# Moving the last block of transposes behind the u projection, and nine weight sums from GpSimd to VectorE, in a hybrid encoder layer on one Trainium2 core

## The chip, the cores and the metric

The kernel runs on one core of one Trainium2 chip. A core has a matrix engine (TensorE, PE in the profile; PEld is its weight load), a vector engine (VectorE, DVE), a scalar engine (ScalarE, ACT), a programmable engine (GpSimd, POOL) and a sync engine (SyncE, SP) whose queue issues the weight transfers. Each engine works through its own queue in program order, and waits there for what its next instruction needs. The metric is the time of one launch on the device in microseconds (us).

## What is computed

One layer of an encoder, for one sequence of 512 positions and 1024 channels in fp32; the feed-forward width is 2816.

```
h  = rmsnorm(x, g_pre_mix)
q, k, v, g, u, sv, a_ret, a_sgu = split(h @ w_in)       # widths 512 512 1024 1024 1024 1024 1024 1024
o  = layernorm(retention_forward(q, k, v) + retention_backward(q, k, v))
ret = (o * silu(g)) @ w_ret_o
sv = layernorm(gelu(sv));  mixed = w_spatial @ sv (chunks of 128) + b_spatial
sgu = (gelu(u) * mixed) @ w_sgu_o
x1 = x + rmsnorm((sigmoid(a_ret) * ret + sigmoid(a_sgu) * sgu) @ w_out, g_post_mix)
hid = conv3(rmsnorm(x1, g_pre_ffn) @ w_up) + conv_b;  a, b = split(hid)
out = x1 + rmsnorm((gelu(a) * b) @ w_down, g_post_ffn)
```

## The kernel before

**Precision.** Every fp32 matmul is done as three matmuls on halves: `split` makes a high part by an ACT copy (L95) and the low part by a DVE subtraction (L102), and PE multiplies high by high, high by low and low by high. Weights and activations both go through it. A weight block arrives as a raw tile (512 KB, SP's queue, four buffers tagged `raw`), and its high and low parts go into one of nine slots (tag `w4`). `w_get` takes the next unit of a list, `units`, and issues the transfers and splits of the following units ahead of their use, as far as its look-ahead allows.

**Stages.** The wide groups (`t_group`, L541 to L543) come first and make q, k, v, sv and g with the positions on the partitions. The last of them makes the second half of g; `g_evac(acc, 1)` applies Silu to it and multiplies it into the second half of the retention output, `o_sb[t, 1]`, four row blocks of 128 positions (DVE, L676). `last_turn` then transposes these: 16 transposes of 128x128 on PE (L685) into four PSUM banks, row block by row block, with two matmuls in between that sum the spatial weights over a row (L688, into `rws`). ACT and DVE split each bank into `gh` and `gl`, the second half of the left operand of the product with `w_ret_o`.

**The u stage.** Then come four pairs of output blocks for u, class `Pair`. A pair makes a 2x2 arrangement of half blocks with seven products in place of eight, from weights named B11, B21, T1, T2, T3, T4 and B22 and activations x (two halves) and the sums S1 to S4, which are made once. The weights' sums are T1 = B11 + B12 and T3 (DVE, L178 and L179, named by their lines in the profile), T2 = T1 + B22 (GpSimd, L180) and T4 = T2 + B21 (GpSimd, L182). Each of the seven products is twelve matmuls of 128x256 (L756). `part1` issues x·B11, x·B21, S1·T1 and S2·T2, with T2's product accumulating on B11's bank after ACT has copied that bank out; `part2` issues S3·T3, on the same bank again after a further copy; `part3` issues the remaining two. `part3` of a pair is issued after `part1` of the next pair. DVE combines the results (L773, L778, L784, L793, L796, L798), and ACT applies Gelu (L799). The first pair's first product is ordered behind `last_turn`'s last instruction by `tc.issue_after(turned)`.

**Behind it.** `gated_pair` makes a further pair with Sigmoid, `a_ret`, and two whole blocks (`f_block`, L229 to L231) of the product with `w_ret_o`, eight steps of three matmuls of 128x512 each; the steps five to eight read the last `gh` and `gl`. The fourth u pair's `part3` is issued after the first gated pair's `part1`.

**The up-projection.** Later the feed-forward's up-projection runs in couples: a pair and two whole blocks. The pair's T2 and T4 are GpSimd's as above; the results go through the convolution (L1028, L1031, L1035) and the Gelu (L1042).

The order within each engine's queue is made by a scheduler from the program's order and its dependences, and `tc.issue_after` adds an order on one engine.

Of the kernel before, what the change touches and what calls it, by code (L numbers as in the profile page):

```python
# [13 lines left out]
ALU = mybir.AluOpType  # L14

P = 128
D = 1024
S = 512
NT = S // P
# [8 lines left out]
U0, GATE0, GATE1 = 32, 40, 72  # L28
# [8 lines left out]
UP0 = DOWN0 - 2 * NF  # L37
EARLY = 4
COUPLES = [(i, i + 1) for i in range(4, 20, 2)]
# [8 lines left out]
def tile_block(ctx: ExitStack, tc, xT, x, wall, par, cs, wsp, bsp, gpost, gffn, out):  # L48
    nc = tc.nc
# [6 lines left out]
    def nm(s):  # L56
        uid[0] += 1
        return f"{s}_{uid[0]}"

    def blk(dt=F32, n="blk", shape=(P, S)):  # L60
        return sb.tile(list(shape), dt, tag="blk", bufs=NBLK, name=nm(n))
# [17 lines left out]
    def tmp(n="tmp", shape=(P, S)):  # L79
        return sb.tile(list(shape), F32, tag="tmp", bufs=6, name=nm(n))  # L80
# [7 lines left out]
    def ps(shape=(P, S)):  # L88
        return pp.tile(list(shape), F32, tag="ps", name=nm("ps"))

    def const(n, shape):
        return sb.tile(list(shape), F32, tag=n, bufs=1, name=n)

    def copy(o, i):
        return nc.scalar.activation(out=o, in_=i, func=AF.Copy)  # L95

    def as32(t):
        return t.bitcast(F32)

    def split(hi, lo, src):  # L100
        copy(hi, src)
        nc.vector.tensor_sub(lo, src, as32(hi))  # L102
# [6 lines left out]
    units = []  # L109
    i = 0  # L110
    while i < NW:
        pair = [(f, i) for f in FORMS]
        if U0 <= i < GATE0:
            units += pair
            i += 2
        elif GATE0 <= i < GATE1:
            units += pair[:4] + [("blk", i + 2)] + pair[4:] + [("blk", i + 3)]
            i += 4
        elif i == UP0 + 2 * COUPLES[0][0]:
            for a, b in COUPLES:  # L120
                pair = [(f, UP0 + 2 * a) for f in FORMS]
                units += pair[:4] + [("blk", UP0 + 2 * b)] + pair[4:] + [("blk", UP0 + 2 * b + 1)]
            i = UP0 + 2 * COUPLES[-1][1] + 2
        elif i == DOWN0:
            for _ in range(2):
                pairs = [[("q", i + j), ("t", i + j)] for j in range(DP)]
                whole = [[("blk", i + DP)], [("blk", i + DP + 1)]]
                for u in pairs[:4] + whole[:1] + pairs[4:6] + whole[1:] + pairs[6:] if i == DOWN0 else pairs + whole:
                    units += u
                i += DP + WHOLE // 2  # L130
        else:
            units.append(("blk", i))
            i += 1
    w_ready, w_pos, w_held, w_raw = {}, [0, 0], [0], {}

    def raw_tile():
        return sb.tile([P, 1024], F32, tag="raw", bufs=4, name=nm("raw"))
# [4 lines left out]
    def slot(n, at=0, w=1024):  # L142
        return sb.tile([P, 1088], F32R, tag="w4", bufs=9, name=nm(n))[:, at : at + w]
# [23 lines left out]
    def w_form(form, i):  # L167

        if form == "B11":
            a, b = raw_tile(), raw_tile()  # L170
            nc.sync.dma_start(a, wall[i])
            nc.sync.dma_start(b, wall[i + 1])
            w_raw["B11"], w_raw["B12"] = a[:, :S], a[:, S:]
            w_raw["B22"], w_raw["B21"] = b[:, :S], b[:, S:]
        elif form == "T1":
            t = raw_tile()
            w_raw["T1"], w_raw["T2"], w_raw["T3"], w_raw["T4"] = t[:, :S], t[:, S:], w_raw["B12"], t[:, S:]
            nc.vector.tensor_add(w_raw["T1"], w_raw["B11"], w_raw["B12"])  # L178
            nc.vector.tensor_add(w_raw["T3"], w_raw["B12"], w_raw["B22"])  # L179
            nc.gpsimd.tensor_tensor(out=w_raw["T2"], in0=w_raw["T1"], in1=w_raw["B22"], op=ALU.add)  # L180
        elif form == "T4":
            nc.gpsimd.tensor_tensor(out=w_raw["T4"], in0=w_raw["T2"], in1=w_raw["B21"], op=ALU.add)  # L182
        w = slot("wf", 0, 1088)
        lo, hi = w[:, AT_64 : AT_64 + S], w[:, S + AT_192 : 2 * S + AT_192]
        split(hi, lo, w_raw[form])
        return hi, lo
# [50 lines left out]
    T0, T1 = slice(0, 256), slice(256, 512)  # L237
# [88 lines left out]
    for k in range(KD):  # L326
# [10 lines left out]
        if k == 0:  # L337
            for half in range(2):
                for f in (T0, T1) if half == 0 else (slice(0, S),):
                    for a, b in ((wh, xh), (wl, xh), (wh, xl)):  # L340
                        for m in range(4 * half, 4 * half + 4):
                            nc.tensor.matmul(  # L342
                                qk[m][:, f], a[:, m * P : (m + 1) * P], b[0][:, f],
                                start=a is wh and b is xh and f.start == 0, stop=False, skip_group_check=True,
# [27 lines left out]
    ident = const("ident", [P, P])  # L372
# [14 lines left out]
    for t in range(NT):  # L387
        for n in range(2):
# [3 lines left out]
                out=xt, in_=xt, func=AF.Square, accum_out=ss[:, 4 * n + t : 4 * n + t + 1]  # L392
# [10 lines left out]
    v = nc.vector  # L403
# [9 lines left out]
    for c in range(19, 1, -2):  # L413
        v.scalar_tensor_tensor(
            out=lc, in0=lc, scalar=1.0 / c, in1=lb, op0=ALU.add, op1=ALU.mult
        )
    v.scalar_tensor_tensor(out=lc, in0=lc, scalar=1.0, in1=la, op0=ALU.add, op1=ALU.mult)
    with behind():
        v.tensor_scalar(out=lg, in0=lgt, scalar1=0.0, scalar2=None, op0=ALU.min)
    v.scalar_tensor_tensor(  # L420
        out=lg, in0=lc, scalar=-2.0, in1=lg, op0=ALU.mult, op1=ALU.add
# [5 lines left out]
    for m in range(8):  # L427
        t = blk(n="qkraw")
# [8 lines left out]
    for t in range(NT):  # L437
# [4 lines left out]
            start=True,  # L442
            stop=True,
# [120 lines left out]
    o_sb = {}  # L564
# [107 lines left out]
    def g_evac(acc, nh):  # L672
        for t in range(NT):
            g = tmp("g")
            nc.scalar.activation(out=g, in_=acc[t], func=AF.Silu, scale=rstd[:, t : t + 1])
            v.tensor_mul(o_sb[t, nh], o_sb[t, nh], g)  # L676
        if nh == 0:
            transposed([o_sb[t, nh] for t in range(NT)], ogh, ogl)

    def last_turn():  # L680

        p, rw = [ps() for _ in range(4)], ps()
        for t in range(NT):
            for f in range(4):
                i = nc.tensor.transpose(p[f][:, t * P : (t + 1) * P], o_sb[t, 1][:, f * P : (f + 1) * P], ident)  # L685
            if t > 1:
                with tc.issue_after(i.ins):
                    i = nc.tensor.matmul(rw, ones, wst_parts[t - 2], start=t == 2, stop=t == 3)  # L688
        for f in range(4):
            h_, l_ = blk(F32R, "gh"), blk(F32R, "gl")  # L690
            split(h_, l_, p[f])
            ogh.append(h_)
            ogl.append(l_)
        copy(rws, rw)
        return i.ins

# [14 lines left out]
    ones, one = blk(F32R, "ones", (P, P)), blk(n="one", shape=(P, P))  # L711
# [3 lines left out]
    wst_parts = blk(F32R, "wsth"), blk(F32R, "wstl")  # L715
    split(*wst_parts, wst)
    rws = lo64("rws", F32)
    for n, acc in enumerate(t_group()):
        if n < 2:
            for k in (n + 2, n + 6):  # L720
                t = tmp("xT")
# [2 lines left out]
            x_forms(n + 2)  # L724
    sv_norm()
    g_evac(acc, 1)
    turned = last_turn()

    def f_block(ah, al, n, between=None):

# [9 lines left out]
    class Pair:  # L740
# [8 lines left out]
        def product(self, b, act, first, w=None):  # L749
            wh, wl = w or w_get()  # L750
            o = self.b[b][:, T0]
            for k in range(4):
                c = slice(k * P, (k + 1) * P)
                h_, l_ = act(k)
                for n, (w_, a_) in enumerate(((wh, h_), (wh, l_), (wl, h_))):
                    nc.tensor.matmul(  # L756
                        o, w_[:, c], a_, start=first and k == n == 0, stop=k == 3 and n == 2,
                        skip_group_check=True,
                    )
            return o  # L760
# [4 lines left out]
        def s(self, n):  # L765
            return lambda k: self.forms[n][k]

        def part1(self):
            c0, c1 = self.t
            o = self.product(0, self.x(0, T0), True)  # L770
            copy(c0[:, T0], o)
            o = self.product(1, self.x(4, T0), True)
            v.tensor_add(c0[:, T0], o, c0[:, T0])  # L773
            self.product(2, self.s("S1"), True)
            o = self.product(0, self.s("S2"), False)
            copy(c1[:, T0], o)
            if self.scale is not None:
                v.tensor_mul(c0[:, T0], c0[:, T0], self.scale[:, T0])  # L778

# [24 lines left out]
    uT, late = [], None  # L804
    U_HOMES = [lambda: lo64("u", F32), lambda: hi192("u", F32)] + [lambda: blk(n="u")] * 2 + [lambda: hi192("u", F32)] * 4
    for j in range(KD // 2):
        p = Pair(AF.Gelu_apprx_tanh, lambda: U_HOMES.pop()(), None, rbc)
        with tc.issue_after(turned) if j == 0 else ExitStack():
            p.part1()
        if late:  # L810
            late.part3()
        p.part2()
        late = p
        uT += p.t
# [32 lines left out]


    def gated_pair(ah, al, late=None):
        p = Pair(AF.Sigmoid, lambda: tmp("sig"), None, rbc)  # L850
        p.part1()
        if late:
            late.part3()
        o = [f_block(ah, al, KD)]
        p.part2()
        o.append(f_block(ah, al, KD, p.part3))
        return zip(o, p.t)

    r = []
    for j in range(KD // 2):  # L860
        for o, t in gated_pair(ogh, ogl, late if j == 0 else None):
            b = (lo64("r", F32) if j == 0 else hi192("r", F32) if j < 3 else blk(n="r"))
            v.tensor_mul(b, o, t)
            r.append(b)
        mix(2 * j)
        mix(2 * j + 1)
    mh, ml = [], []
    for j in range(KD // 2):
        for i, (o, t) in enumerate(gated_pair(yh, yl)):
            v.tensor_mul(t, o, t)  # L870
            nc.gpsimd.tensor_tensor(out=t, in0=t, in1=r[2 * j + i], op=ALU.add)
            h_, l_ = blk(F32R, "mh"), blk(F32R, "ml")
# [141 lines left out]
    rows2, _ = turn(2, zs[2])  # L1014
    for e in range(1, EARLY):
        early(e, 0)
    _, last3 = turn(3, zs[3])
# [88 lines left out]
    i = 0  # L1106
    while i < NF:
        if i in couples:
            p = Pair(None, lambda: tmp("c"), (h2h, h2l, h2forms))
            p.part1()  # L1110
            o = [f_block(h2h, h2l, KD)]
# [5 lines left out]
        else:  # L1117
            o = []
# [50 lines left out]
    late = list(range(EAGER, DP))  # L1169
# [20 lines left out]
    for j in range(DP):  # L1190
# [5 lines left out]
        if j in (3, 5):  # L1196
            w = w_get()
# [214 lines left out]
```

## Time and profile before

| what | value |
|---|---|
| median of 3 runs | 823.45 us |
| lowest, highest | 822.37, 824.98 us |
| the profiled execution | 821.76 us |
| its span in the trace | 820.0 us |
| its mean granted TensorE clock | 0.998 |
| u stage, last wide matmul to first gated block | 211.8 to 259.2 us |

The span is the time from the first to the last instruction in the trace; the profiled execution's own time lies 1.8 us above it. All positions in the text are microseconds from the span's start. In a row of a timeline stand the start, the length, the engine, the line, the operation, the tiles written and read, the shape and the number of instructions in the row; what follows in brackets is the engine's idle time before it and what ended that. A row of several instructions runs from the first one's start to the last one's end. Matmuls overlap in a pipeline, so a single one's length (0.28 us for 128x256) is more than its share of the time: the distance between starts tells that.

### The profile page before, as it was taken

To read this page: it belongs to the slowest core of one execution; us is meant where nothing else is said; L and a number is where in the kernel's file an instruction comes from. 1 tells how busy PE (TensorE), PEld (TensorE's weight loads), DVE (VectorE), ACT (ScalarE), POOL (GpSimd) and SP (SyncE) were. 2 spreads that over 40 slices of the span, in tenths; PEclk is the share of its full clock that TensorE was granted. 3 is DMA by queue.
4 is the path that set the end of the run, shared out by engine and by line. 5 is a ranking of instruction groups with operands and counts; after the bars stand their busy time and mean duration, and the time that the engine had idled before them with its cause. 6 is when DMAs were issued, how large, how long until landed. Compare 5 with 4: busy or idle time off the path is not lost.

```text
span 820.0 us, 13286 instructions
## 1 busy us (share of the span) xinstructions
PE 809.1 (99%) x5158; PEld 729.0 (89%) x5158; DVE 661.7 (81%) x1107; ACT 441.0 (54%) x777; POOL 101.6 (12%) x102
## 2 busy tenths in 40 slices
PE   9999999999999999999999999999999999999996
PEld 7888888888899999999988898889999998999996
DVE  7489898778898777767765559898889989997967
ACT  6636445536665444444445676565656666555531
POOL 0010000102221111132211210210201200000001
PEclk9999999999999999999999999999999999999999
DMA  8733222212223332233359111333333351223344
GB/s 293 251 116 109 72 78 78 77 53 78 97 97 130 104 104 93 88 103 104 113 164 339 45 56 57 104 103 104 103 104 103 103 181 52 78 104 104 107 151 155
DMA packets 29647, 93.24 MB, mean 114 GB/s; under 512 B 3536, under 2 KB 4432, under 8 KB 29584
## 3 DMA queue, kind: packets, MB, share of 16 engines
q1 hardware_dynamic: 27360, 86.76, 31.6%
q0 software_dynamic: 1360, 4.46, 1.5%
q10 hardware_dynamic: 864, 1.18, 0.4%
q8 instruction: 40, 0.66, 0.3%
q14 instruction: 23, 0.19, 0.1%
HBM read 88.19 MB, written 4.19 MB: 113 GB/s over the span
## 4 chain that ended last, share of the span: by engine, by line
PE 89%; DVE 7%; ACT 2%; issue 1%; DMA 1%; POOL 0%; DVEq 0%; SPq 0%; ACTq 0%; POOLq 0%
PE ps L756 19%; PE ps L230 11%; PE ps L229 11%; PE ps L231 11%; PE ps L1145 11%; PE ps L542 5%; PE ps L541 5%; PE ps L543 5%; PE ps L1161 2%; DVE wf L102 2%; PE ps L903 2%; PE ps L902 2%; PE ps L901 2%; PE ps L826 1%; PE ps L342 1%
## 5 line engine op out<-in xcount | busy, mean ns | idle before, releaser
L102 DVE TENSOR_TENSOR wl<-raw,wh 128x1024 fp32r<-128x1024 f32 (+1 forms) x92 | 107.4, 1175 | 45.5 <-PE ps L756 20.4
L95 ACT ACTIVATE wf<-raw 128x512 fp32r<-128x512 f32 x140 | 84.9, 626 | 100.1 <-PE ps L230 39.7
L102 DVE TENSOR_TENSOR wf<-raw,wf 128x512 fp32r<-128x512 f32 x140 | 112.1, 811 | 20.4 <-ACT wf L95 19.4
L756 PE MATMUL ps<-sh,wf 128*128 128x256 f32 x640 | 119.3, 277 | 1.2 <-ACT c L95 1.0
L95 ACT ACTIVATE wh<-raw 128x1024 fp32r<-128x1024 f32 (+2 forms) x96 | 93.4, 983 | 39.9 <-DMA raw<-wall 16.8
L756 PEld LDWEIGHTS ps<-sh,wf 128*128 128x128 f32 x640 | 100.9, 188 | 2.5 <-ACT c L95 1.2
L230 PE MATMUL ps<-h2l,wh 128*128 128x512 f32 (+1 forms) x256 | 92.6, 363 | 0.0
L229 PE MATMUL ps<-h2h,wh 128*128 128x512 f32 (+1 forms) x256 | 92.6, 364 | 0.0
L231 PE MATMUL ps<-h2h,wl 128*128 128x512 f32 (+1 forms) x256 | 92.4, 362 | 0.0
L756 PE MATMUL ps<-sl,wf 128*128 128x256 f32 x320 | 88.5, 276 | 0.0
L541 PE MATMUL ps<-wh,xh 128*128 128x512 f32 x192 | 75.0, 391 | 0.0
L542 PE MATMUL ps<-wl,xh 128*128 128x512 f32 x192 | 74.9, 390 | 0.0
L543 PE MATMUL ps<-wh,xl 128*128 128x512 f32 x192 | 74.8, 390 | 0.0
L180 POOL TENSOR_TENSOR raw<-raw,raw 128x512 f32<-128x512 f32 x20 | 36.7, 1835 | 236.6 <-DVE raw L178 208.4
L756 PEld LDWEIGHTS ps<-sl,wf 128*128 128x128 f32 x320 | 60.1, 188 | 0.6
L1145 PE MATMUL ps<-dl,fh 128*128 128x256 f32 x216 | 59.8, 277 | 0.0
L1145 PE MATMUL ps<-dh,fh 128*128 128x256 f32 x216 | 59.7, 277 | 0.0
L1145 PE MATMUL ps<-dh,fl 128*128 128x256 f32 x216 | 59.7, 277 | 0.0
L231 PEld LDWEIGHTS ps<-h2h,wl 128*128 128x128 f32 x256 | 48.1, 188 | 7.7
L229 PEld LDWEIGHTS ps<-h2h,wh 128*128 128x128 f32 x256 | 47.8, 188 | 7.1 <-ACT h2h L971 0.3
L230 PEld LDWEIGHTS ps<-h2l,wh 128*128 128x128 f32 x256 | 48.1, 188 | 6.6
L756 PE MATMUL ps<-xh,wf 128*128 128x256 f32 x288 | 53.5, 278 | 0.0
(314 smaller groups left out, 2045.3 us busy)
## 6 DMA issues: line engine op xcount, KB each, us to landing
raw<-wall SPq DMA_DIRECT2D x144, 512.0 KB, 3.6
x<-x SPq DMA_DIRECT2D x24, 256.0 KB, 5.8
x<-x POOLq DMA_DIRECT2D x8, 256.0 KB, 2.3
xT<-xT SPq DMA_DIRECT2D x7, 256.0 KB, 5.3
xT<-xT POOLq DMA_DIRECT2D x4, 256.0 KB, 3.6
out<-zg SPq DMA_DIRECT2D x4, 256.0 KB, 2.0
raw<-wall SPq DMA_DIRECT2D x3, 256.0 KB, 4.8
out<-zs ACTq DMA_DIRECT2D x3, 256.0 KB, 3.8
```

Source lines behind the costliest of these rows:

```text
L95: return nc.scalar.activation(out=o, in_=i, func=AF.Copy)
L102: nc.vector.tensor_sub(lo, src, as32(hi))
L180: nc.gpsimd.tensor_tensor(out=w_raw["T2"], in0=w_raw["T1"], in1=w_raw["B22"], op=ALU.add)
L229: nc.tensor.matmul(o, ah, bh, start=start, stop=False, skip_group_check=skip)
L230: nc.tensor.matmul(o, ah, bl, start=False, stop=False, skip_group_check=skip)
L231: nc.tensor.matmul(o, al, bh, start=False, stop=stop, skip_group_check=skip)
L541: nc.tensor.matmul(acc[t], xh[k][:, c], wh[:, f], start=k == 0, stop=False)
L542: nc.tensor.matmul(acc[t], xh[k][:, c], wl[:, f], start=False, stop=False)
L543: nc.tensor.matmul(acc[t], xl[k][:, c], wh[:, f], start=False, stop=k == KD - 1)
L756: nc.tensor.matmul(o, w_[:, c], a_, start=first and k == n == 0, stop=k == 3 and n == 2, skip_group_check=True,)
L901: nc.tensor.matmul(o, ah, bh, start=k == 0, stop=False)
L1145: nc.tensor.matmul(o, a_[:, c], w_[:, f], start=j == t == i == 0, stop=j == DP - 1 and i == 2 and n not in (M2, M3, M4), skip_group_check= ...
```

## The change

There are three edits. The turn: the two weight sums (`row_sums`) alone follow the last wide group, and u's first product is ordered behind them; the transposes and their splits come in two parts, `last_turn((0, 1))` behind the fourth u pair's `part2`, and `last_turn((2, 3))` behind the first gated pair's `part1`, before the fourth u pair's `part3`. The first pair: its B21 product is issued after T2's, and its units are listed in that order. The sums: T2 and T4 of the four u pairs, and T2 of the first up-projection couple, are DVE's. The engines' instruction counts stay as they were, but for these nine sums, which leave GpSimd for DVE.

```
         if U0 <= i < GATE0:
-            units += pair
+            units += [pair[n] for n in (0, 2, 3, 1, 4, 5, 6)] if i == U0 else pair
...
-            nc.gpsimd.tensor_tensor(out=w_raw["T2"], in0=w_raw["T1"], in1=w_raw["B22"], op=ALU.add)
+            eng = nc.vector if i < GATE0 or i == UP0 + 2 * COUPLES[0][0] else nc.gpsimd
+            eng.tensor_tensor(out=w_raw["T2"], in0=w_raw["T1"], in1=w_raw["B22"], op=ALU.add)
         elif form == "T4":
-            nc.gpsimd.tensor_tensor(out=w_raw["T4"], in0=w_raw["T2"], in1=w_raw["B21"], op=ALU.add)
+            eng = nc.vector if i < GATE0 else nc.gpsimd
+            eng.tensor_tensor(out=w_raw["T4"], in0=w_raw["T2"], in1=w_raw["B21"], op=ALU.add)
...
-    def last_turn():
+    def last_turn(fs):
 
-        p, rw = [ps() for _ in range(4)], ps()
-        for t in range(NT):
-            for f in range(4):
-                i = nc.tensor.transpose(p[f][:, t * P : (t + 1) * P], o_sb[t, 1][:, f * P : (f + 1) * P], ident)
-            if t > 1:
-                with tc.issue_after(i.ins):
-                    i = nc.tensor.matmul(rw, ones, wst_parts[t - 2], start=t == 2, stop=t == 3)
-        for f in range(4):
+        for f in fs:
+            p = ps()
+            for t in range(NT):
+                i = nc.tensor.transpose(p[:, t * P : (t + 1) * P], o_sb[t, 1][:, f * P : (f + 1) * P], ident)
             h_, l_ = blk(F32R, "gh"), blk(F32R, "gl")
-            split(h_, l_, p[f])
+            split(h_, l_, p)
             ogh.append(h_)
             ogl.append(l_)
+        return i.ins
+
+    def row_sums():
+
+        rw = ps()
+        for n, w in enumerate(wst_parts):
+            i = nc.tensor.matmul(rw, ones, w, start=n == 0, stop=n == 1)
         copy(rws, rw)
         return i.ins
...
-    turned = last_turn()
+    summed = row_sums()
...
-        def part1(self):
+        def part1(self, apart=False):
+
             c0, c1 = self.t
+
+            def second():
+                o = self.product(1, self.x(4, T0), True)
+                v.tensor_add(c0[:, T0], o, c0[:, T0])
+
             o = self.product(0, self.x(0, T0), True)
             copy(c0[:, T0], o)
-            o = self.product(1, self.x(4, T0), True)
-            v.tensor_add(c0[:, T0], o, c0[:, T0])
+            if not apart:
+                second()
             self.product(2, self.s("S1"), True)
             o = self.product(0, self.s("S2"), False)
             copy(c1[:, T0], o)
+            if apart:
+                second()
...
-        with tc.issue_after(turned) if j == 0 else ExitStack():
-            p.part1()
+        with tc.issue_after(summed) if j == 0 else ExitStack():
+            p.part1(j == 0)
...
     def gated_pair(ah, al, late=None):
+
         p = Pair(AF.Sigmoid, lambda: tmp("sig"), None, rbc)
-        p.part1()
         if late:
-            late.part3()
+            with tc.issue_after(late.last.ins):
+                turned = last_turn((0, 1))
+            with tc.issue_after(turned):
+                p.part1()
+            with tc.issue_after(p.last.ins):
+                turned = last_turn((2, 3))
+            with tc.issue_after(turned):
+                late.part3()
+        else:
+            p.part1()
```

`product` keeps its last matmul as `self.last` for these orders.

More of the change, by code (lines that the diff above doesn't have):

```diff
@@ L755, in product @@
                 for n, (w_, a_) in enumerate(((wh, h_), (wh, l_), (wl, h_))):
-                    nc.tensor.matmul(
+                    self.last = nc.tensor.matmul(
                         o, w_[:, c], a_, start=first and k == n == 0, stop=k == 3 and n == 2,
```

## The prediction

> **What bounds the kernel now.** I read the page's busy times and its chain first, then the busy windows of the stretches that the change touches, then the timelines of single engines there.
>
> ```profile
> span 820.0 us, 13286 instructions
> ## 1 busy us (share of the span) xinstructions
> PE 809.1 (99%) x5158; PEld 729.0 (89%) x5158; DVE 661.7 (81%) x1107; ACT 441.0 (54%) x777; POOL 101.6 (12%) x102
> ...
> PE 89%; DVE 7%; ACT 2%; issue 1%; DMA 1%; POOL 0%; DVEq 0%; SPq 0%; ACTq 0%; POOLq 0%
> ```
>
> PE is busy for 809.1 of 820.0 us and carries 89% of the chain. The change adds no matmul and takes none away, so it can win only moments in which PE stands still, and lose only by making new ones. All that can be won is therefore small. The question is which stalls lie where the edits reach. The windows (time, PE, PEld, DVE, ACT, POOL busy, granted clock, DMA share, GB/s) show the u stage whole, ten us of it, and the stretch around the first couple:
>
> ```profile
> 211.80:259.20 47.40, 46.93 (x403) 46.08 (x402) 42.34 (x66) 30.62 (x58) 10.28 (x7) 1.00 0.32 106
> 230.00:240.00 10.00, 10.00 (x90) 10.00 (x90) 9.89 (x16) 6.66 (x13) 2.60 (x3) 1.00 0.32 107
> ...
> 508.00:525.00 17.00, 15.98 (x95) 14.01 (x94) 14.63 (x24) 8.61 (x15) 4.71 (x2) 1.00 0.18 56
> ```
>
> The granted clock is 1.00 in each, so the clock explains nothing here. VectorE (DVE) is close behind PE: 9.89 of 10 us in the middle of the u stage. That makes it the engine to watch when sums are moved to it. "Busy" for PE hides stalls under a microsecond, because overlapping records count as busy; I therefore compare start times. First the turn (start, length, instruction, wait):
>
> ```profile
> 211.81 1.47 PE L685 MATMUL ps<-ident,o 128*128 128x128 f32 x12
> 213.04 0.48 PE L688 MATMUL ps<-wsth,ones 128*128 128x512 f32 x1
> 213.79 0.65 PE L685 MATMUL ps<-ident,o 128*128 128x128 f32 x4 [0.27 <-DVE o L676]
> 214.20 0.48 PE L688 MATMUL ps<-wstl,ones 128*128 128x512 f32 x1
> 214.52 0.28 PE L756 MATMUL ps<-xh,wf 128*128 128x256 f32 x1
> ...
> 219.98 0.28 PE L756 MATMUL ps<-xh,wf 128*128 128x256 f32 x1
> ```
>
> From 214.52 to 219.98 there are 48 matmuls of 128x256 (four products of twelve): 0.114 us each. Twelve transposes take 213.04 - 211.81 = 1.23 us, 0.103 each. A weight sum streams 512 columns where a product's matmul streams 256, so I put it at twice 0.114, 0.23 us. The u stage has 16 transposes, 2 sums and 384 product matmuls: 1.64 + 0.46 + 43.7 = 45.8 us. It takes 47.40, so no more than 1.6 us can be won there, whatever the mechanism.
>
> **The change part by part: the turn.** Before, it fills 211.81 to 214.52, 2.71 us, for 1.64 + 0.46 = 2.10 us of work: 0.61 us is standing still, most of it until DVE has multiplied the last row block of o (0.27 shown as a wait, 0.75 between starts where a sum needs 0.23). After, the two sums stand alone behind the last wide product, and u's first product starts at about 211.81 + 0.46 = 212.3. The 16 transposes come back at the end of the stage, when o has long been ready; they cost their 1.64 us again, and two more changes between transposes and products. The change at 214.20 cost 0.32 - 0.23 = 0.09 us, so two cost up to 0.2. Gain 0.4 to 0.6 us; I take **0.45**. The wait for o is not replaced: what the first product now needs is its weights and a bank that ScalarE (ACT) has evacuated, and both came before 214.52 without a wait in the row; whether they come before 212.3 the row does not say, so the lower bound is a loss of this gain.
>
> **The second product put behind T2.** The pair's accumulating bank must be copied out by ACT between S2·T2 and the next product on it. These are the places where PE waits for that copy, and the copies:
>
> ```profile
> 220.21 0.39 PE L756 MATMUL ps<-xh,wf 128*128 128x256 f32 x2
> 220.62 0.38 PE L756 MATMUL ps<-sh,wf 128*128 128x256 f32 x1
> ...
> 244.66 0.28 PE L756 MATMUL ps<-sh,wf 128*128 128x256 f32 x1
> 245.12 0.38 PE L756 MATMUL ps<-sh,wf 128*128 128x256 f32 x1 [0.18 <-ACT u L95]
> ```
>
> ```profile
> 220.18 0.38 ACT L95 ACTIVATE u<-ps 128x256 f32<-128x256 f32 x1 [0.73 <-PE ps L756]
> ...
> 244.69 0.37 ACT L95 ACTIVATE u<-ps 128x256 f32<-128x256 f32 x1
> ```
>
> At 220.62 the first pair loses 0.41 - 2 x 0.114 = 0.18 us, and the restarted matmul is 0.10 longer than its 0.28: 0.28 in all. Four matmuls of the second pair already stood in between and hid the rest. With the whole B21 product there, 12 x 0.114 = 1.37 us cover a copy of 0.38 that starts at once: **0.28** goes. But T2 itself now comes one product earlier after B11, whose copy it needs; one product (S1·T1, 1.37 us) remains between them. That covers 0.38 us unless the copy is held up in ACT's queue by a us. T1's and T2's weights are wanted one product earlier too, and the list of units moves them up by as much.
>
> **The sums on VectorE.** How a GpSimd (POOL) sum stands to DVE's work is seen in a pair of views, POOL's timeline and DVE's:
>
> ```profile
> 224.88 1.78 POOL L180 TENSOR_TENSOR raw<-raw,raw 128x512 f32<-128x512 f32 x1 [4.15 <-DMA raw<-wall]
> ```
>
> ```profile
> 224.82 0.69 DVE L179 TENSOR_TENSOR raw<-raw,raw 128x512 f32<-128x512 f32 x1 [0.88 <-DMA raw<-wall]
> 225.43 1.78 DVE L102 TENSOR_TENSOR wf<-raw,wf 128x512 fp32r<-128x512 f32 x1
> ```
>
> While POOL adds, a DVE operation of the same size takes 1.78 us where its neighbour takes 0.69. The window of the stage counts 7 sums on POOL. If each lengthens one DVE operation by 1.09, and the sum on DVE itself costs 0.61 (start to start, 225.43 - 224.82), DVE is relieved by 7 x 0.48 = 3.4 us, and T2 and T4 are ready about 1.1 us sooner. If the long DVE operations have another cause, DVE gains nothing and carries 7 x 0.61 = 4.3 us more. I take the relief, since the long operation starts inside the POOL sum. The Trainium skill, "SBUF — State Buffer", section "Who interferes with whom", says that DVE and GpSimd contend for a shared port pair held for a whole instruction, so that the later one fully blocks. This trace agrees in direction: 1.78 against 0.69; by a full block the DVE operation, which would start after 226.66, would end at 227.35 instead of the measured 227.21, which alters no term of the sum.
>
> What this wins on PE is the stall at 245.12: 0.46 - 0.11 = 0.35, and 0.10 of restart, 0.45 us, because the copy at 244.69 came late through ACT's queue, which stood behind DVE. Bounds 0 and 0.45; I take **0.4**, and 0.1 for the slower matmuls in the rest of the stage. So the u stage wins 0.45 + 0.28 + 0.4 + 0.1 = 1.23 of the 1.6 us possible.
>
> **The one later sum.** Here the chain, engine by engine (POOL; ACT; DVE; PE):
>
> ```profile
> 510.90 3.42 POOL L180 TENSOR_TENSOR raw<-raw,raw 128x512 f32<-128x512 f32 x1 [30.37 <-DVE raw L178]
> ```
>
> ```profile
> 514.36 0.63 ACT L95 ACTIVATE wf<-raw 128x512 fp32r<-128x512 f32 x1 [2.92 <-POOL raw L180]
> ...
> 518.91 0.63 ACT L1042 ACTIVATE cv<-cv 128x512 f32<-128x512 f32 x1 [1.78 <-DVE cv L1035]
> ...
> 520.11 1.66 ACT L95 ACTIVATE wf<-raw 128x512 fp32r<-128x512 f32 x3
> 521.67 0.37 ACT L95 ACTIVATE c<-ps 128x256 f32<-128x256 f32 x1
> ```
>
> ```profile
> 515.54 0.69 DVE L102 TENSOR_TENSOR sl<-h,sh 128x512 fp32r<-128x512 f32 x1 [2.37 <-ACT sh L95]
> ```
>
> ```profile
> 520.79 0.28 PE L756 MATMUL ps<-sh,wf 128*128 128x256 f32 x1
> 522.09 0.39 PE L756 MATMUL ps<-sh,wf 128*128 128x256 f32 x1 [1.02 <-ACT c L95]
> ```
>
> POOL needs 3.42 us; ACT waits for it (2.92), DVE waits for ACT (2.37), and all behind them comes late until PE waits for the copy of c: 522.09 - 520.79 - 0.11 = 1.19, with 0.11 of restart **1.30** us. On DVE the sum takes 0.61 to 0.69 in place of 3.42. It still stands behind the DVE operations already queued between 510.9 and 513.1, which themselves move back by 0.6; DVE then has an idle gap of 2.37 us that this fills. I expect the chain about 1.9 us earlier: the copy at 519.8, done by 520.2, while PE wants the bank at 520.9. Cover 0.7 us, so the whole 1.30 goes; the bounds are 0 and 1.30. The next couple keeps its POOL sum but gets an earlier start:
>
> ```profile
> 532.96 0.39 PE L231 MATMUL ps<-h2h,wl 128*128 128x512 f32 x1
> 533.36 0.39 PE L756 MATMUL ps<-h2h,wf 128*128 128x256 f32 x1
> ```
>
> Between these, 0.40 - 0.23 + 0.11 = 0.28 are lost; I count **0.2**, bounds 0 and 0.28.
>
> **The moved splits.** The second half's four ACT copies and four DVE subtractions leave the start of the stage and come at its end, where the first gated block needs them. DVE's row there:
>
> ```profile
> 259.06 0.69 DVE L178 TENSOR_TENSOR raw<-raw 128x512 f32<-128x512 f32 x1 [2.44 <-DMA raw<-wall]
> ```
>
> DVE stands idle for 2.44 us, as long as four subtractions (4 x 0.61). So I cost them at nothing. The cover fails where the last two stand in DVE's queue behind this waiting L178: queues are in order, and behind L178 wait these two, and for them the gated block, the last k-steps of its eight, 3 x 0.23 us each.
>
> **Sum.** 1.23 + 1.30 + 0.2 = 2.73 us. The profiled execution took 821.76 us (span 820.0), and should come to about 819.0; the median of the runs, 823.45, lies 1.7 above it and should come to **820.7**.
>
> **The rivals.** *Only the first stage wins* (chance 0.24): at the first couple another wait takes the place. For it: DVE has 14.63 of 17 us there, and ACT at 518.91 waited for DVE's convolution, not for the sum. Against: DVE's idle 2.37. Then 1.23 and some tenths, 1.4: 822.0.
>
> *The gated block waits for the last gl* (0.12): L178's transfer lands no earlier than before, so L178 runs at 259.06. With it, a split of twice the width and three more operations ahead, and the two subtractions themselves, eight times 0.61, the last one ends at 263.9. The block starts where the stage ends, 259.2 - 1.2 = 258.0, and reaches its eighth k-step 7 x 0.69 us later, at 262.8. PE loses 1.1: net gain 1.6, 821.8.
>
> *VectorE becomes the bound: slower* (0.12). The long DVE operations are not POOL's doing, and 4.3 us come on top in a stage where DVE is at 9.89 of 10. Of its idle 47.40 - 42.34 = 5.1 us only the 2.44 at the end can be filled, and the gl subtractions want that same gap, so PE runs 4.3 us late and none of the 1.23 is won; the couple still wins 1.30: +3.0, 826.4. It decides once DVE's work for a pair passes PE's 84 matmuls, 9.6 us. Against it: long DVE operations and POOL sums coincide. The Trainium skill, "Perfetto Trace Analysis", section "Optimizing Scalar/DVE Operations", speaks for this rival: where DVE is saturated, offloading some work even to GPSIMD may make sense, and the change does the reverse; its next sentence, that the two share a read port, so that moving between them might not help, weakens it, and the 1.78 against 0.69 agrees with that one.
>
> *It does nothing* (0.04): each stall returns one instruction later: 823.4.
>
> **Numbers.** The forecast has 0.48. A measurement here tells about 0.3%, 2.5 us, so faster means below 821.0, slower above 825.9. The forecast's own bounds: no less than 819.5 with everything won (1.6 + 1.30 + 0.28 = 3.2, and 0.7 for the scatter of the runs), and 821.4 with half of the 1.30. Faster: most of the forecast's 0.48, and a little of the first rival: 0.50. Slower: 0.11. Same: the rest, 0.39. The range goes from 819.3 to 823.9; beyond it lie the slower case and the tail of a larger gain.
>
> **What would show it.** Right: u's first product 0.5 us behind the last wide product instead of 2.7; no gap over 0.15 us on PE until the transposes; DVE operations of 128x512 at 0.69 throughout the u stage, and a stage of about 46.2 us; PE without the gap near 521; the gated block without a wait for gl. Wrong: DVE rows still at 1.7 with POOL idle, PE waiting for wf in the u stage, or a gap of over 1 us around the first couple under another releaser.

## The result, and the profile after

The changed kernel took 822.30 us (median of 15 runs, 819.92 to 823.20) where the kernel before took 825.35 (822.25 to 827.60) beside it. The medians differ by 3.05 us; the ratio of the two sets of runs is 0.9958, 95% interval 0.9945 to 0.9971, which is some 3.5 us. Two later comparisons gave 0.9974 (0.9962 to 0.9986) and 0.9963 (0.9950 to 0.9976). The prediction was 820.7 for 823.45, a ratio of 0.9967. But the one profiled execution of the changed kernel is longer than that of before: 822.30 us against 821.76, spans 820.5 and 820.0. What hides the gain there is told below. First the page of the changed kernel, the busy times and the chain:

```profile
PE 810.8 (99%) x5158; PEld 731.9 (89%) x5158; DVE 657.8 (80%) x1116; ACT 441.6 (54%) x777; POOL 85.2 (10%) x93
...
PE 91%; DVE 5%; DMA 2%; issue 1%; ACT 0%; POOL 0%; DVEq 0%; SPq 0%; ACTq 0%
```

DVE has nine operations more (1116 for 1107) and is busy 3.9 us less. The windows of the two stretches (time, PE, PEld, DVE, ACT, POOL, clock, DMA share, GB/s):

```profile
230.00:240.00 10.00, 10.00 (x90) 10.00 (x90) 8.78 (x18) 6.27 (x13) 0.00 (x0) 1.00 0.32 107
508.00:525.00 17.00, 17.00 (x100) 14.99 (x100) 16.92 (x28) 10.16 (x19) 1.29 (x1) 1.00 0.26 93
```

In the u stage DVE now does 18 operations in 8.78 us where 16 took 9.89. At the couple PE is busy for all of the 17 us. The groups of DVE and POOL operations by shape between 212 and 260 us say why, first those of before, then those of the changed kernel (line, operation, count, then busy us and mean ns):

```profile
L102 DVE TENSOR_TENSOR wf<-raw,wf 128x512 fp32r<-128x512 f32 x28 | 24.1, 871 | 0.5 <-ACT wf L95 0.3
...
L182 POOL TENSOR_TENSOR raw<-raw,raw 128x512 f32<-128x512 f32 x4 | 5.3, 1317 | 17.5 <-DVE wf L102 17.5
L180 POOL TENSOR_TENSOR raw<-raw,raw 128x512 f32<-128x512 f32 x3 | 5.0, 1672 | 12.6 <-DMA raw<-wall 12.6
```

```profile
L102 DVE TENSOR_TENSOR wf<-raw,wf 128x512 fp32r<-128x512 f32 x28 | 19.9, 724 | 2.7 <-ACT wf L95 2.6
...
L181 POOL TENSOR_TENSOR raw<-raw,raw 128x512 f32<-128x512 f32 x2 | 2.6, 1323 | 62.1 <-ACT wf L95 62.1
L184 POOL TENSOR_TENSOR raw<-raw,raw 128x512 f32<-128x512 f32 x1 | 1.3, 1288 | 3.8 <-DVE wf L102 3.8
```

The same 28 subtractions take 4.2 us less. The three sums that are left on GpSimd in this window belong to the gated pairs, which the change does not touch. The turn, on PE's timeline of the changed kernel:

```profile
213.04 0.39 PE L545 MATMUL ps<-wh,xl 128*128 128x512 f32 x1
213.26 0.39 PE L698 MATMUL ps<-wsth,ones 128*128 128x512 f32 x1
213.49 0.39 PE L698 MATMUL ps<-wstl,ones 128*128 128x512 f32 x1
213.72 0.28 PE L761 MATMUL ps<-xh,wf 128*128 128x256 f32 x1
```

u's first product starts 0.46 us behind the end of the wide group. At the couple (DVE, then ACT):

```profile
512.42 0.68 DVE L181 TENSOR_TENSOR raw<-raw,raw 128x512 f32<-128x512 f32 x1
```

```profile
513.13 0.63 ACT L95 ACTIVATE wf<-raw 128x512 fp32r<-128x512 f32 x1 [0.58 <-DVE raw L181]
...
519.39 0.37 ACT L95 ACTIVATE c<-ps 128x256 f32<-128x256 f32 x1
```

The sum takes 0.68 us for 3.42, ACT waits 0.58 for it in place of 2.92, and the copy of c is out at 519.8, ahead of PE. The moved subtractions:

```profile
256.53 0.69 DVE L178 TENSOR_TENSOR raw<-raw 128x512 f32<-128x512 f32 x1 [1.41 <-DMA raw<-wall]
257.14 1.22 DVE L102 TENSOR_TENSOR wl<-raw,wh 128x1024 fp32r<-128x1024 f32 x1
258.28 1.28 DVE L102 TENSOR_TENSOR gl<-ps,gh 128x512 fp32r<-128x512 f32 x2
```

The transfer came 2.5 us earlier than before, and the last gl is written at 259.6, long before the gated block's seventh step.

And here is what was not foreseen, in the last projection, PE and DVE:

```profile
759.49 0.28 PE L1167 MATMUL ps<-dh,fl 128*128 128x256 f32 x1
760.24 0.38 PE L1167 MATMUL ps<-dh,fh 128*128 128x256 f32 x1 [0.48 <-DVE e L1201]
...
761.44 0.38 PE L1167 MATMUL ps<-dh,fh 128*128 128x256 f32 x1 [0.23 <-DVE yy L1202]
```

```profile
755.57 0.69 DVE L199 TENSOR_TENSOR raw<-raw 128x512 f32<-128x512 f32 x1 [1.72 <-DMA raw<-wall]
...
759.51 0.68 DVE L1201 TENSOR_TENSOR e<-ps,uu 128x512 f32<-128x512 f32 x1
...
760.71 0.68 DVE L1202 TENSOR_TENSOR yy<-ps,e 128x512 f32<-128x512 f32 x1
```

DVE waits 1.72 us for a weight transfer; behind it in the queue stand the reads (L1201, L1202) that free PSUM banks, and PE waits for those twice. What follows is worse, seen by counting matmuls in a window of the tail, before and after:

```profile
766.00:806.00 40.00, 40.00 (x355) 40.00 (x354) 31.21 (x56) 14.94 (x22) 0.56 (x1) 1.00 0.35 120
```

```profile
766.00:806.00 40.00, 40.00 (x342) 40.00 (x342) 30.25 (x55) 14.52 (x20) 0.56 (x1) 1.00 0.35 117
```

PE is busy for 40.00 of 40 us in both and the granted clock is 1.00 in both, but 342 matmuls pass where 355 did: 0.117 us each for 0.113. No row shows a gap; only the count does.

The table takes the distance between the starts of the same matmuls in each trace; e1 to e8 are the experiments of the next section, before_again, after_again and after_third are repeats of the two kernels. Its rows are the start-up, the u stage from the last wide matmul to the gated block, the first couples, the down-projection around 760 us, and the tail. The stretches in between agree within 0.7 us.

| us (position before) | before | before_again | e1 | e2 | e3 | e4 | after | after_again | after_third | e5 | e6 | e7 | e7_again | e8 |
|---|---|---|---|---|---|---|---|---|---|---|---|---|---|---|
| start-up (1 to 20) | 19.0 | 20.9 | 21.4 | 21.3 | 19.4 | 19.5 | 20.5 | 20.4 | 19.2 | 20.8 | 21.2 | 18.9 | 20.3 | 21.2 |
| u stage (211.6 to 259.2) | 47.63 | 48.87 | 46.71 | 47.02 | 48.63 | 47.85 | 46.11 | 46.36 | 46.36 | 47.87 | 46.36 | 46.36 | 46.36 | 48.02 |
| couples (505 to 538) | 33.02 | 33.50 | 33.14 | 32.71 | 31.38 | 31.40 | 31.38 | 31.38 | 31.38 | 31.49 | 31.38 | 31.61 | 31.38 | 32.95 |
| around 760 (754 to 764.5) | 10.50 | 10.50 | 10.98 | 11.47 | 11.28 | 11.25 | 11.66 | 11.68 | 11.86 | 11.26 | 10.50 | 10.50 | 10.50 | 10.50 |
| tail (764.5 to 812) | 47.54 | 47.54 | 49.32 | 49.32 | 49.32 | 49.32 | 49.32 | 49.32 | 47.54 | 49.32 | 47.54 | 47.54 | 47.54 | 47.54 |

The first profile after was 1.5 us late out of the start-up, then won 1.5 in the u stage, 0.3 up to the couples and 1.6 there, and lost 1.2 at 760 and 1.8 in the tail.

### The profile page after: what moved, and what is told of

Read it like the earlier page. It is cut to its first block, busy times and chain, and to the rows that moved or that the text cites. A ratio compares the mean times of both kernels' runs of the same rounds, so it can differ in the third digit from the quotient of the medians.

```text
span 820.5 us, 13278 instructions
## 1 busy us (share of the span) xinstructions
PE 810.8 (99%) x5158; PEld 731.9 (89%) x5158; DVE 657.8 (80%) x1116; ACT 441.6 (54%) x777; POOL 85.2 (10%) x93
## 4 chain that ended last, share of the span: by engine, by line
PE 91%; DVE 5%; DMA 2%; issue 1%; ACT 0%; POOL 0%; DVEq 0%; SPq 0%; ACTq 0%
PE ps L761 23%; PE ps L231 13%; PE ps L232 12%; PE ps L233 12%; PE ps L1167 6%; PE ps L544 5%; PE ps L543 5%; PE ps L545 5%; PE ps L923 2%; PE ps L924 2%; PE ps L925 2%; DMA raw<-wall 1%; DVE dl L102 1%; PE ps L344 1%; PE ps L839 1%
## 5 line engine op out<-in xcount | busy, mean ns | idle before, releaser
L102 DVE TENSOR_TENSOR wl<-raw,wh 128x1024 fp32r<-128x1024 f32 (+1 forms) x92 | 107.3, 1174 | 48.7 <-PE ps L761 24.2
L102 DVE TENSOR_TENSOR wf<-raw,wf 128x512 fp32r<-128x512 f32 x140 | 106.2, 770 | 25.3 <-ACT wf L95 24.5
L181 POOL TENSOR_TENSOR raw<-raw,raw 128x512 f32<-128x512 f32 x15 | 25.9, 1726 | 239.0 <-DVE raw L178 170.0
```

The source lines that it names most:

```text
L181: eng.tensor_tensor(out=w_raw["T2"], in0=w_raw["T1"], in1=w_raw["B22"], op=ALU.add)
```

## The experiments

**e1: the turn and the first pair's order alone.** All sums on GpSimd:

```
-            eng = nc.vector if i < GATE0 or i == UP0 + 2 * COUPLES[0][0] else nc.gpsimd
+            eng = nc.gpsimd
...
-            eng = nc.vector if i < GATE0 else nc.gpsimd
+            eng = nc.gpsimd
```

> The turn and the first pair's order alone, all sums on GpSimd as before. My account: the stall of the turn (0.5 us) and that of the first pair's copy (0.28) go; the stall near 245 (0.45), the one at the first couple (1.30) and the next couple's (0.28) stay, somewhat moved, and DVE operations of 128x512 beside a GpSimd sum still take 1.7 to 1.8 us. About 0.8 to 1.0 us faster than before. Rival (VectorE's load sets the u stage, the turn's moment is given back later in the stage): the stage's end lies where it was, within 0.2 us, and no gain. If it gains over 2 us, the sums were not what mattered.

Ratio 0.9991 (0.9977 to 1.0006), some 0.7 us, which the interval does not tell from nothing. The turn's stall and the first pair's are gone; the others are there, as PE's timeline shows:

```profile
244.36 0.74 PE L761 MATMUL ps<-sh,wf 128*128 128x256 f32 x2
...
523.14 0.38 PE L761 MATMUL ps<-sh,wf 128*128 128x256 f32 x1 [1.00 <-ACT c L95]
```

Near 244.6 two matmuls take 0.74 for 0.39, 0.35 us lost, and 523.14 is 1.27 us behind its predecessor. The u stage is 46.71, 0.92 less than in the first profile of before. So the turn is not given back later in the stage; the rival falls.

**e2: the u pairs' sums alone.** On the kernel before:

```
-            nc.gpsimd.tensor_tensor(out=w_raw["T2"], ...
+            (nc.vector if i < GATE0 else nc.gpsimd).tensor_tensor(out=w_raw["T2"], ...
```

and T4 likewise.

> T2 and T4 of the four u pairs on VectorE, nothing else of the change. My account: no DVE operation of 128x512 over 0.8 us between 216 and 257 us, DVE busy about 3 us less there, the stall near 245 goes, the turn's and the first pair's stay: 0.4 to 0.6 us faster. Rival (VectorE becomes the bound): PE waits for wf in the u stage, up to 4 us slower. Rival (the sums as such do nothing, the reorder did it): the stall near 245 stays, 0.0.

Ratio 1.0007 (0.9990 to 1.0024): the time decides nothing. The trace does: two long operations on DVE in place of seven, no stall near 245, the turn's 0.53 and the first pair's 0.27 still there, no wait for wf, u stage 47.02. VectorE does not become the bound. Its relief is smaller than expected, though: from 216 to 257 us it is busy 37.16 us for 38.44, 1.3 less and not 3. The two long operations stand beside two sums that GpSimd still does, at 246.32 and 251.44: they are T2 and T4 of the gated pair, which neither e2 nor the change moves.

**e3: the couple's sum alone.** T2 on VectorE only where `i == UP0 + 2 * COUPLES[0][0]`.

> T2 of the first up-projection couple alone on VectorE. My account: the stall near 522 (1.30 us) goes and with it the next couple's (0.28): 1.3 to 1.6 us faster; the u stage as before. Rival (DVE, 14.6 of 17 us busy there, pays for it): a gap of 0.5 us or more under another releaser between 515 and 535, gain below 0.8.

Ratio 0.9983 (0.9967 to 0.9999). Neither stall of the couples is left, 31.38 us as in the changed kernel: 1.3 to 2.1 less than in the five traces that have POOL's sum (32.71 to 33.50). No other releaser took the place.

**e4: the first pair's order as before,** everything else changed:

```
-            units += [pair[n] for n in (0, 2, 3, 1, 4, 5, 6)] if i == U0 else pair
+            units += pair
...
-            p.part1(j == 0)
+            p.part1()
```

> All of the change but the first pair's order: its B21 product stands second again. My account: PE waits for ACT's copy before S3·T3 of the first pair, 0.2 to 0.5 us, and everything else is as in the changed kernel: 3.0 us faster than before, 0.3 slower than the whole change. Rival (without the turn's splits in ACT's queue the copy is in time, and the order is not needed): no gap, the same time as the whole change.

Ratio 0.9989 (0.9974 to 1.0005): 0.9 us where 3.0 were expected. The stage tells where most of the difference went. PE's timeline, then the windows of e4, of the changed kernel and of before_again (a repeat of the kernel before), in that order:

```profile
218.34 0.39 PE L761 MATMUL ps<-xh,wf 128*128 128x256 f32 x2
218.75 0.39 PE L761 MATMUL ps<-sh,wf 128*128 128x256 f32 x1
```

```profile
219.00:248.00 29.00, 29.00 (x246) 29.00 (x246) 26.26 (x46) 18.70 (x35) 1.90 (x2) 1.00 0.33 110
```

```profile
219.00:248.00 29.00, 29.00 (x258) 29.00 (x258) 26.86 (x49) 19.19 (x35) 1.34 (x1) 1.00 0.33 110
```

```profile
219.00:248.00 29.00, 29.00 (x244) 28.80 (x244) 27.35 (x42) 18.79 (x35) 7.89 (x6) 1.00 0.29 92
```

The stall is the expected 0.3 us (0.41 between starts where 0.23 is due, and a longer first matmul). But behind it PE goes on at 0.119 us from start to start, where 0.1133 is its usual distance, until about 250 us and without a gap: 246 matmuls in the window for 258, twelve fewer in 29 us, 1.4 us. The stage is 47.85, 1.5 to 1.7 over the changed kernel's. In before_again the same slow stretch runs from the turn to the end of the stage, in e3 from the first pair's stall on. In the first profile of before it was nearly absent. And the first pair's stall does not always bring it: in e2 and e8 PE is slow from the turn on, and goes on at 0.1133 behind that very stall. So the 1.4 us are what followed the stall in e4, not a fixed price.

**after_again and before_again: the two kernels once more.**

> The changed kernel once more, for what its first profile holds by chance. If the late start (PE at half pace until 8.6 us) and the long transfer near 740 us were chance, the start is sound here and the span is 1 to 3 us shorter; if they belong to the change, both are there again. On the stall at 760 us: in five of six profiles so far, with and without the change, PE waits there for VectorE and then keeps a pace of 0.118 us per matmul to the end; expected here too, about 3 us in all.

Ratio 0.9974 (0.9962 to 0.9986). The late start was there again (20.4), and in after_third not (19.2): chance. The wait near 760 and the slow tail were there again.

> The kernel before once more. If its first profile was a lucky one, PE now waits near 760 us for VectorE (0.4 to 1.2 us) and goes on at 0.118 us per matmul where it had 0.1133, and the span is 2 to 4 us longer than 820.0. The stalls of the turn (0.5), of the first pair (0.28), near 245 (0.45) and near 522 (1.30) are there again, each within 0.15 us; if they move about by more, single profiles don't bear the account.

The span was 823.2, but not by the late wait: it is absent in both profiles of before. The four stalls are there in kind; near 522 it was 1.6, and near 245 the slow stretch took the stall's place. By the test that the expectation sets, then, a single profile does not bear the sizes.

**e5: GpSimd beside VectorE.** After each of the eight sums:

```
+    def beside(a, b):
+        for n in range(4):
+            c = slice(n * 112, (n + 1) * 112)
+            nc.gpsimd.tensor_tensor(out=idle, in0=a[:, c], in1=b[:, c], op=ALU.add)
```

> The changed kernel, and beside each of the u pairs' eight sums GpSimd adds the same operands once more, in four pieces of 112 columns, into a tile that nobody reads. If GpSimd's additions as such lengthen VectorE's operations, operations of 128x512 over 1.2 us come back in the u stage, VectorE has now the sums and the long operations and passes 95% of the stage, and PE stalls again: 0.5 to 3 us slower than the changed kernel. If the long operations had another cause (the place of the sum in VectorE's queue), they stay at 0.69 and the time stays.

Ratio 0.9999 (0.9985 to 1.0014), u stage 47.87: the gain is gone. POOL's and DVE's timelines:

```profile
235.85 3.31 POOL L171 TENSOR_TENSOR idle<-raw,raw 128x112 f32<-128x112 f32 x4 [2.83 <-DVE raw L184]
```

```profile
236.29 0.92 DVE L185 TENSOR_TENSOR raw<-raw,raw 128x512 f32<-128x512 f32 x1
237.12 0.91 DVE L187 TENSOR_TENSOR raw<-raw,raw 128x512 f32<-128x512 f32 x1
237.96 0.91 DVE L102 TENSOR_TENSOR wf<-raw,wf 128x512 fp32r<-128x512 f32 x1
...
244.78 0.69 DVE L184 TENSOR_TENSOR raw<-raw 128x512 f32<-128x512 f32 x1 [0.99 <-POOL idle L171]
```

Beside a piece of 112 columns a DVE operation takes 0.92 us for 0.69: 0.23 more, 2.1 ns a column. Beside a sum of 512 columns it took 1.09 more, also 2.1 ns a column. Twelve DVE operations between 211 and 239 us take 0.91 to 0.92 us. So POOL's work as such lengthens DVE's operations, and the loss goes with its size. Not every piece does it: at 242.77 a subtraction (L102) takes 0.69 among POOL's pieces. The expected lengths over 1.2 us did not come, because the pieces are small. The loss of time is not DVE's alone: it waited 0.99 and 0.32 us until POOL had read a raw tile, a wait that the added reads brought in. The experiment shows the lengthening, not its price.

**e7, and e7_again: the reads that free banks first.** The sums of one later weight block go behind them in DVE's queue; the order is put on the first of the three, and the other two read its result:

```
+            with tc.issue_after(gate[0]) if i == DOWN0 + DP + WHOLE // 2 + 2 else ExitStack():
                 nc.vector.tensor_tensor(
...
-        v.tensor_sub(yy, m[M5], e1)
+        gate.append(v.tensor_sub(yy, m[M5], e1).ins)
```

> The changed kernel with one addition: three VectorE sums for a later weight block, which wait near 755 us for a transfer, are ordered behind the operation that frees the PSUM bank PE waits for. If the wait at 760 us is VectorE's queue standing behind that transfer, it goes, and if the slow pace to the end comes from that stall, it goes too: 1.1 + 1.9 = 3.0 us faster than the changed kernel. If the slow pace has a cause of its own, only 0.5 to 1.2. If the weight block now comes late, PE waits for it near 765 us, and nothing is gained or up to 2 us lost.

Ratio 0.9944 (0.9927 to 0.9961), median 820.27, 2.3 us under the changed kernel's 822.58 on the same chip, where 3.0 were expected. DVE's timeline and the tail:

```profile
755.56 0.68 DVE L1204 TENSOR_TENSOR e<-ps,uu 128x512 f32<-128x512 f32 x1
...
756.76 0.69 DVE L1205 TENSOR_TENSOR yy<-ps,e 128x512 f32<-128x512 f32 x1
```

```profile
766.00:806.00 40.00, 40.00 (x355) 40.00 (x355) 30.84 (x54) 14.82 (x22) 1.00 (x2) 1.00 0.38 119
```

The reads come 4 us earlier in the trace, 3 of them against PE's own place, PE waits for neither, and the tail has its 355 matmuls.

> e7 once more, beside e8 on the same chip: no wait near 760 us, 0.1133 us per matmul to the end (47.5 us for the tail), about 3.9 us faster than e8 and 2 to 3 faster than the changed kernel.

Ratio 0.9943 (0.9929 to 0.9957), median 819.80, again without the wait.

> The changed kernel beside e7 and e8: with the wait near 760 us and the slow tail (49.3 us) in most runs, 2 to 3 us slower than e7; u stage 46.1 to 46.4, first couples 31.4.

Ratio 0.9963 (0.9950 to 0.9976), median 821.44: 1.6 us over e7 on the same chip, less than expected. The wait was there (11.86), and this time the tail kept its pace (47.54): the wait makes the slow tail likely, not certain.

**e8: the kernel before with e7's reordering.**

> The kernel before with the one reordering of e7 (three sums for a later weight block behind the operation that frees PE's bank), nothing of the change. It takes the late wait and its slow tail out of both sides of the comparison. If that wait is chance and falls on both kernels alike, this kernel is about 1.5 us faster than before (it was in none of two profiles of before and in two of three of its single-edit versions), and e7 beats it by what the u stage and the couple gain, 2.1 + 1.8 = 3.9 us. If the wait belongs to the change, this kernel equals before, and e7 beats it by about 4 too, while the change alone loses 3 of that.

Ratio 0.9991 (0.9981 to 1.0002), 0.7 us, about half of what was expected and within no gain. Against it e7_again is 0.9943 / 0.9991 = 0.9952, 4.0 us faster: with the late wait out of both, the change is worth what the table says, some 2.0 us in the u stage (47.63 to 48.87 without any of its edits there, 46.11 to 46.36 with all) and 1.3 to 2.1 at the couples. (The expectation counts the wait in two of three single-edit versions; by the table it was in all three, e1, e2 and e3.)

**e6: all later sums on VectorE.** Its file contains e7's reordering as well, which the expectation doesn't say, so it is to be read against e7.

> The changed kernel, and the other fifteen T2 and T4 sums of the up-projection couples on VectorE too. My account: PE has no wait left in those couples, so nothing can be won; VectorE, busy 34.0 of 35 us at 505 to 540 and 69.8 of 80 after, gains 1.1 - 0.6 us per sum. Same time as the changed kernel within 0.3 us. If VectorE is past its bound there, PE waits for wf between 505 and 700 us and the kernel is slower by up to 1 us.

Ratio 0.9954 (0.9942 to 0.9967) against e7_again's 0.9943 beside it: no gain, no loss that can be told. The couples stay at 31.38 and PE waits nowhere for wf.

## Why the prediction was right, point by point

**What bounds the kernel** was right: PE, and only its stalls could be won. **The turn** was right, 0.46 us to the first product. **The sums** were right in mechanism: the long operations were POOL's doing (871 to 724 ns, e2, e5), and each sum on DVE costs less than it frees. The size of the relief was misread: of the seven sums that the prediction counts in the stage, the last two (245.45 and 250.32) are the gated pair's and stay on GpSimd (242.85 and 248.03 in the changed kernel), and DVE's busy time in the stage fell from 42.57 to 41.16 us, 1.4 and not 3.4. The forecast's gain on PE did not hang on that size: e1 and e2, which divide the stage's edits, gain 0.92 and 0.61 us against the first profile of before, where 0.73 and 0.5 were forecast. The Trainium skill, "SBUF — State Buffer", section "Summary: rules for kernel authors", has the second of the two to issue blocked until the first has finished, if the VectorE operation has two inputs in SBUF and GpSimd's reads SBUF. e5 agrees in that the loss grows with GpSimd's columns, 0.23 us to 1.09; but 0.23 is less than the 0.42 us that a piece is recorded with where DVE stands idle (244.33), and there the measurement decides.

**The later sum** was right, 1.5 us forecast for both couples, 1.3 to 2.1 measured. **The moved splits** cost nothing, as forecast: the gated block did not wait, and the feared L178 ran 2.5 us earlier because its transfer did.

**Two steps were off.** The first is "no more than 1.6 us can be won there, whatever the mechanism". That bound took one profile for the rule. Against that profile it held, 47.63 to 46.11, 1.5 us for the 1.23 forecast; but other traces with the stage as it was need up to 1.2 us more, because PE can stay at 0.118 to 0.119 us per matmul for tens of microseconds behind a stall. The mis-sized term is the first pair's stall, "0.28 in all", which counts the gap and the restart and nothing behind them: in e4 it came with 1.5 to 1.7. That is one trace, and in e2 and e8 no slow stretch followed the same stall.

The second is that the sum ended at the couples. In all three profiles of the changed kernel PE waited at 760 us, 1.2 to 1.4 us, and in two of them went slow to the end, 1.8 more. e7 against the changed kernel on the same chips puts the average at 1.6 to 2.5 us. The two errors have opposite signs: about 4.0 us won, and 1 to 2 lost once the 0.7 that the kernel before loses at the same place (e8) is taken off, against 2.7 forecast. That is why the total came out close: the stages won by the mechanisms that were forecast, but that their surplus and the late wait nearly cancel is luck. The changed kernel's profiled execution was forecast at 819.0 and took 822.30.

Whether the change makes the late wait more likely stays open. It hangs on one transfer, issued some 12.4 us ahead of the same point on PE's timeline (754.1 before) in every trace: it took 3.3 and 3.5 us in the two profiles of before, and 4.5 to 5.1 in all twelve others, among them e2, e3 and e8, which leave the turn as it was. By e8's 0.7 us the kernel before loses less by it than the changed one; two short and three long transfers among the kernels with the old turn are too few to say why.

**The rivals.** *VectorE becomes the bound* fell: 8.78 of 10 us for 9.89, and at the couple 16.92 of 17 us busy without a wait on PE. *Only the first stage wins* and *the gated block waits* fell by e3 and by the rows of gl, *it does nothing* by the ratio. That something given back later would eat a part of the gain was the first rival's shape, but its place was 230 us further on than it looked.

## What to carry to other kernels

Moving work off a slow engine onto a busier one can relieve the busier one, if the two hinder each other: look for operations that take longer than their neighbours of the same shape, and for who runs beside them. A stall can cost more than its gap: count matmuls per window, since a busy share of 100% at full clock can hide a pace that is 4 to 5% slow. And before a gain is promised from one profile, take a second one of the same kernel; here the start-up (18.9 to 21.4 us) and the wait near 760 us with its tail (up to 3.1 us) together move the span by more than the change does.

## What the runs showed of the hardware

After a stall of 0.2 to 0.8 us PE often ran 128x256 matmuls at 0.1178 to 0.119 us in place of 0.1133, for 30 us or to the end of the kernel, with the granted clock at 1.00; after others of the same size it did not, and in e2 and e8 the first pair's stall ended the slow pace. What holds it there was not found. A GpSimd addition, where it lengthened a VectorE operation of 128x512, did so by up to about 2.1 ns for each of GpSimd's columns (0.23 us for 112, 1.09 for 512). And the same weight transfer at the same point of PE's program took 3.3 or 5.1 us, in different executions.
